# Linear attention on one core: V buffers cleared by two engines behind the first loads, the last group in another order, and two groups' stores on SyncE's queue

## The chip, the cores and the metric

The kernel runs on one core of a Trainium2 chip. The core's engines are TensorE (PE, with its weight loads shown as PEld), VectorE (DVE), ScalarE (ACT), GpSimd (POOL) and SyncE (SP); they work side by side and wait for one another through semaphores. Data move between the chip's memory (HBM) and the on-chip buffers by DMA, which an engine asks for and 16 DMA engines carry out. The metric is device time in microseconds, the median of several runs.

## The reference

For each of 8 x 12 heads, with 512 rows of 64 elements in float32:

```python
Q_feat = np.maximum(0, Q) + 1
K_feat = np.maximum(0, K) + 1
KV = np.einsum('bhkd,bhkv->bhdv', K_feat, V)
K_sum = np.sum(K_feat, axis=2)
numerator = np.einsum('bhqd,bhdv->bhqv', Q_feat, KV)
denominator = np.einsum('bhqd,bhd->bhq', Q_feat, K_sum)
return (numerator / (denominator[:, :, :, None] + 1e-10)).astype(np.float32)
```

That is attention without a softmax: one 64 x 64 product of K and V a head, applied to every row of Q and divided by a row sum. Inputs are 3 x 12.6 MB and the output 12.6 MB.

## The kernel before, in words

The rows are laid out over 128 partitions, and the work is cut into NG = 12 groups of 8 heads. A group goes through these steps:

- `load(g)`: K, Q and V come in by DMA and are turned from float32 to bfloat16 on the way; only K of group 0 comes as float32, through SP's queue. All other loads are asked for by POOL, as 1 DMA for K, 4 for V and 1 for Q. The four V pieces of 32 partitions each go into four diagonal blocks of a large tile `v_blk` (5 blocks of 2 x 16 x 64 elements); what lies off the diagonal must be zero, and the fifth block holds ones at four columns (the copy at L196), which make the row sums of K in the same matmul. There are NV = 3 such tiles, cleared once at the start on VectorE (L186), and used by groups in turn.
- `features(g)`: max(x + 1, 1) on VectorE, two instructions for K (`kf`) and two for Q (`qf`).
- `keys_values(g)`: 32 matmuls on PE into `kva_ps`, and four copies by ScalarE into a block-diagonal tile `kva_diag` (also three of them, cleared at L188).
- `transposes(g)`: 16 transposes of `qf` on PE into `qt_ps`, and two copies by ScalarE into `qt`.
- `output(g)`: four tiles of matmuls `o_ps` on PE; for each a reciprocal (L172) and a multiply (L173) on VectorE into `o_sb`. Two tiles fit in PSUM at a time, so the third waits for VectorE's multiply of the first.
- `store(g)`: `o_sb` goes out by one DMA of POOL's queue, that of the last group as two halves by SP's queue (L106).

Every engine works through its instructions in the order in which the code at the end of the kernel issues them; nothing reorders them. The loads run AHEAD = 3 groups in front, the stores LAG = 3 groups behind, and both are issued by POOL in one line, so a DMA that has to wait there holds up those behind it. The tile framework adds the waits: a V load waits for the clearing of its tile or for the matmuls that last read it, and POOL has eight semaphores for its DMAs, so that a DMA waits until the eighth before it has landed. In each round of the loop the order is features of g, transposes of g - 1, output of g - 2, keys_values of g, then the load of g + 3 and the store of g - 3. After the loop come the rest of the last three groups and four stores.

Of the kernel before, what the change touches and what calls it, by code (L numbers as in the profile page):

```python
# [8 lines left out]
FP32 = mybir.dt.float32  # L9
BF16 = mybir.dt.bfloat16  # L10
# [5 lines left out]
LAG = 3  # L16
AHEAD = 3
# [3 lines left out]
def kernel(  # L21
# [52 lines left out]
    raw = {}  # L74
    feat = {}
    qts = {}
    outs = {}

    def load(g):
        first = g == 0  # L80
        k_raw = (head_pool if first else in_pool).tile(
            [P, 2, C2, D], FP32 if first else BF16, name="k_raw"
        )
        q_raw = in_pool.tile([P, 2, C2, D], BF16, name="q_raw")
        (nc.sync if first else nc.gpsimd).dma_start(  # L85
            out=k_raw, in_=k_dram[:, g * 2 : g * 2 + 2]
        )
        if first:
            nc.gpsimd.dma_start(out=q_raw, in_=q_dram[:, g * 2 : g * 2 + 2])  # L89
        for b in range(4):  # L90
            nc.gpsimd.dma_start(  # L91
                out=v_blk[g % NV][32 * b : 32 * b + 32, b],
                in_=v_dram[32 * b : 32 * b + 32, 2 * g : 2 * g + 2],
            )
        if not first:
            nc.gpsimd.dma_start(out=q_raw, in_=q_dram[:, g * 2 : g * 2 + 2])  # L96
        raw[g] = (k_raw, q_raw)

    def store(g):
        o_sb = outs.pop(g)  # L100
        o_to = o_dram[:, g * NP : g * NP + NP]
        if g < NG - 1:
            nc.gpsimd.dma_start(out=o_to, in_=o_sb)  # L103
            return
        for h in range(2):
            nc.sync.dma_start(out=o_to[:, h:NP:2], in_=o_sb[:, h:NP:2])  # L106

    def feature(dst, src):
        nc.vector.tensor_scalar(  # L109
            out=dst, in0=src, scalar1=1.0, scalar2=1.0, op0=ALU.add, op1=ALU.max  # L110
        )

    def features(g):
        k_raw, q_raw = raw.pop(g)
        kf = feat_pool.tile([P, C2, 2, D], BF16, name="kf")
        qf = feat_pool.tile([P, C2, 2, D], BF16, name="qf")
        for n in range(2):
            feature(kf[:, :, n], k_raw[:, n])
        for half in range(2):
            cs = slice(half * C, half * C + C)  # L120
            feature(qf[:, cs].rearrange("p c n d -> p n c d"), q_raw[:, :, cs])
        feat[g] = (kf, qf)

    def keys_values(g):
        kf, _ = feat[g]
        vb = v_blk[g % NV]
        kva_ps = psum_kva.tile([P, 5, D], FP32, name="kva_ps")
        for c in range(C2):
            for n in range(2):
                nc.tensor.matmul(  # L130
                    kva_ps[64 * n : 64 * n + 64],
                    lhsT=kf[:, c, n, :],
                    rhs=vb[:, :, n, c, :],
                    start=(c == 0),
                    stop=(c == C2 - 1),
                )
        kva = kva_diag[g % NV]
        for n in range(2):
            ps = slice(64 * n, 64 * n + 64)
            nc.scalar.copy(out=kva[ps, :, n, 0:D], in_=kva_ps[ps, 0:4, :])  # L140
            nc.scalar.copy(out=kva[ps, :, n, D], in_=kva_ps[ps, 4, 0:4])  # L141

    def transposes(g):
        _, qf = feat.pop(g)
        qt = mid_pool.tile([P, C, P, 2], BF16, name="qt")
        for half in range(2):
            qt_ps = psum_qt.tile([P, C, P], BF16, name="qt_ps")
            for c in range(C):
                nc.tensor.transpose(qt_ps[:, c, :], qf[:, half * C + c, :, :], identity)  # L149
            nc.scalar.copy(out=qt[:, :, :, half], in_=qt_ps)  # L150
        qts[g] = qt
# [29 lines left out]
        outs[g] = o_sb  # L181

    with tc.manual_schedule():
        nc.vector.memset(ones, 0.0)  # L184
        for t in v_blk:
            nc.vector.memset(t, 0.0)  # L186
        for t in kva_diag:
            nc.vector.memset(t, 0.0)  # L188
        for g in range(AHEAD):
            load(g)  # L190
            if g == 0:
                make_identity(nc, identity)
                for b in range(4):
                    nc.vector.memset(ones[32 * b : 32 * b + 32, b : b + 1], 1.0)
                for t in v_blk:
                    nc.vector.tensor_copy(  # L196
                        out=t[:, 4, :, :, 0:4].rearrange("p n c j -> p (n c) j"),
                        in_=ones[:, None, :].to_broadcast([P, 2 * C2, 4]),
                    )
        for g in range(NG - 1):  # L200
            features(g)
            if g >= 1:
                transposes(g - 1)
            if g >= 2:
                output(g - 2)
            keys_values(g)
            if g + AHEAD < NG:
                load(g + AHEAD)
# [12 lines left out]

# [28 lines left out]
```

## Time and profile before

| | |
|---|---|
| Time before, median of 3 runs | 133.04 us (132.28 to 133.11) |
| Profiled execution | 131.9 us, of which span 130.1 us |
| Granted TensorE clock, mean | 0.834 |
| Busy share PE, PEld, DVE, ACT, POOL | 57%, 41%, 56%, 32%, 39% |
| HBM read and written | 37.75 MB and 12.58 MB |
| First matmul | 19.97 us |
| Last multiply on VectorE ends | 126.47 us |

The profile is one execution. Its times run from the start of the span. "Busy" is time in an instruction; what ended an engine's idle time stands behind an arrow. PEclk is the clock that TensorE was granted, as a share of full speed; the DMA row gives the mean busy share of the 16 DMA engines, and the GB/s row what they moved, counted where the data land or leave on the chip's side of the float32 to bfloat16 turn. In a timeline a row is: start, microseconds from the first to the last of its instructions, engine, line, operation, output and input, count, and in brackets the idle time ahead of it and what ended that.

### The profile page before, as it was taken

To read this page: it belongs to the slowest core of one execution; us is meant where nothing else is said; L and a number is where in the kernel's file an instruction comes from. 1 tells how busy PE (TensorE), PEld (TensorE's weight loads), DVE (VectorE), ACT (ScalarE), POOL (GpSimd) and SP (SyncE) were. 2 spreads that over 40 slices of the span, in tenths; PEclk is the share of its full clock that TensorE was granted. 3 is DMA by queue.
4 is the path that set the end of the run, shared out by engine and by line. 5 is a ranking of instruction groups with operands and counts; after the bars stand their busy time and mean duration, and the time that the engine had idled before them with its cause. 6 is when DMAs were issued, how large, how long until landed. Compare 5 with 4: busy or idle time off the path is not lost.

```text
span 130.1 us, 2367 instructions
## 1 busy us (share of the span) xinstructions
PE 74.2 (57%) x960; PEld 53.4 (41%) x960; DVE 72.7 (56%) x158; ACT 41.4 (32%) x73; POOL 51.4 (39%) x88
## 2 busy tenths in 40 slices
PE   0000008996929785694912992991992896378130
PEld 0000004674816564473811761670662664156120
DVE  4976989237486592928507607705724805990180
ACT  0000030298360739027270045046028019003600
POOL 3093773194618244462462372273273240202000
PEclk9999999999995999689997578568559559959965
DMA  3999999999999999999999999999999999999834
GB/s 86 327 152 154 205 204 203 208 212 207 212 207 212 209 208 211 207 281 303 195 248 336 207 235 348 212 222 358 205 218 354 218 212 377 419 417 413 343 154 178
DMA packets 13914, 32.13 MB, mean 247 GB/s; under 512 B 1360, under 2 KB 1360, under 8 KB 13904
## 3 DMA queue, kind: packets, MB, share of 16 engines
q0 software_dynamic: 13088, 29.89, 98.5%
q1 hardware_dynamic: 816, 2.10, 4.4%
q8 instruction: 7, 0.11, 0.3%
q14 instruction: 3, 0.02, 0.0%
HBM read 37.75 MB, written 12.58 MB: 387 GB/s over the span
## 4 chain that ended last, share of the span: by engine, by line
DMA 51%; DVE 22%; PE 12%; issue 6%; POOL 4%; ACT 2%; ACTq 1%; POOLq 0%
DMA k_raw<-in_K_dram 17%; DMA v_blk<-in_V_dram 15%; DVE v_blk L186 10%; DMA q_raw<-in_Q_dram 9%; PE kva_ps L130 9%; DMA out_dram<-o_sb 9%; DVE o_sb L173 6%; POOL v_blk L91 3%; PE o_ps L162 2%; DVE kf L109 2%; DVE qf L109 1%; DVE recip L172 1%; DVE kva_diag L188 1%; ACT qt L150 1%; PE qt_ps L149 1%
## 5 line engine op out<-in xcount | busy, mean ns | idle before, releaser
L130 PE MATMUL kva_ps<-v_blk,kf 128*64 128x320 bf16 x384 | 42.8, 396 | 20.1 <-DMA q_raw<-in_Q_dram 20.0
L130 PEld LDWEIGHTS <-kf 128*64 128x64 bf16 x384 | 28.3, 147 | 30.5 <-DVE kf L109 20.5
L162 PE MATMUL o_ps<-kva_diag,qt 128*64 128x130 bf16 x384 | 20.9, 249 | 31.2 <-DVE o_sb L173 28.1
L91 POOL DMA_DIRECT2D v_blk<-in_V_dram x48 | 25.8, 544 | 32.5 <-DMA k_raw<-in_K_dram 11.8
L173 DVE TENSOR_TENSOR o_sb<-o_ps,recip 128x512 f32<-128x512 f32 x48 | 33.2, 691 | 1.6
L150 ACT COPY qt<-qt_ps 128x1024 bf16<-128x1024 bf16 x24 | 29.6, 1302 | 0.3
L162 PEld LDWEIGHTS <-qt 128*64 128x64 bf16 x384 | 13.8, 122 | 37.1 <-DVE o_sb L173 32.7
L140 ACT CAST kva_diag<-kva_ps 64x256 bf16<-64x256 f32 x24 | 8.9, 371 | 63.3 <-PE kva_ps L130 62.9
L109 DVE TENSOR_SCALAR qf<-q_raw 128x1024 bf16<-128x1024 bf16 x24 | 9.7, 447 | 30.3 <-DMA q_raw<-in_Q_dram 30.3
L103 POOL DMA_DIRECT2D out_dram<-o_sb x11 | 8.5, 773 | 21.9 <-DVE o_sb L173 10.1
L172 DVE RECIPROCAL recip<-o_ps 128x8 f32<-128x8 f32 x48 | 9.4, 197 | 11.7 <-PE o_ps L162 11.7
L186 DVE MEMSET v_blk<- 128x5120 uint32 x3 | 13.0, 4325 | 3.1 <-issue 3.1
L149 PE MATMUL qt_ps<-identity,qf 128*128 128x128 bf16 x192 | 14.0, 231 | 0.0
L149 PEld LDWEIGHTS <-qf 128*128 128x128 bf16 x192 | 11.9, 104 | 4.2 <-issue 4.2
L109 DVE TENSOR_SCALAR kf<-k_raw 128x1024 bf16<-128x1024 bf16 (+1 forms) x24 | 9.8, 450 | 5.8 <-DMA k_raw<-in_K_dram 3.4
L85 POOL DMA_DIRECT2D k_raw<-in_K_dram x11 | 7.8, 713 | 8.2 <-DMA out_dram<-o_sb 3.7
L96 POOL DMA_DIRECT2D q_raw<-in_Q_dram x11 | 7.9, 716 | 2.9 <-DVE kf L109 1.1
L140 ACT ACT_TABLE_LOAD x1 | 1.3, 1283 | 17.5 <-DVE kva_diag L188 17.5
L141 ACT CAST kva_diag<-kva_ps 64x4 bf16<-64x4 f32 x24 | 4.0, 168 | 0.0
L188 DVE MEMSET kva_diag<- 128x520 bf16 x3 | 1.5, 492 | 0.2
L89 POOL DMA_DIRECT2D q_raw<-in_Q_dram x1 | 0.8, 823 | 0.8 <-POOLq L234 0.8
L184 DVE MEMSET ones<- 128x2 uint32 x1 | 0.1, 60 | 0.8 <-PEq L234 0.8
(8 smaller groups left out, 1.6 us busy)
## 6 DMA issues: line engine op xcount, KB each, us to landing
out_dram<-o_sb POOLq DMA_DIRECT2D x11, 1024.0 KB, 12.0
q_raw<-in_Q_dram POOLq DMA_DIRECT2D x12, 512.0 KB, 10.0
v_blk<-in_V_dram POOLq DMA_DIRECT2D x48, 128.0 KB, 9.2
k_raw<-in_K_dram POOLq DMA_DIRECT2D x11, 512.0 KB, 11.8
k_raw<-in_K_dram SPq DMA_DIRECT2D x1, 1024.0 KB, 4.9
out_dram<-o_sb SPq DMA_DIRECT2D x2, 512.0 KB, 2.7
```

The costliest lines, as they stand in the source:

```text
L91: nc.gpsimd.dma_start(out=v_blk[g % NV][32 * b : 32 * b + 32, b], in_=v_dram[32 * b : 32 * b + 32, 2 * g : 2 * g + 2],)
L96: nc.gpsimd.dma_start(out=q_raw, in_=q_dram[:, g * 2 : g * 2 + 2])
L103: nc.gpsimd.dma_start(out=o_to, in_=o_sb)
L109: nc.vector.tensor_scalar(out=dst, in0=src, scalar1=1.0, scalar2=1.0, op0=ALU.add, op1=ALU.max)
L130: nc.tensor.matmul(kva_ps[64 * n : 64 * n + 64], lhsT=kf[:, c, n, :], rhs=vb[:, :, n, c, :], start=(c == 0), stop=(c == C2 - 1),)
L140: nc.scalar.copy(out=kva[ps, :, n, 0:D], in_=kva_ps[ps, 0:4, :])
L149: nc.tensor.transpose(qt_ps[:, c, :], qf[:, half * C + c, :, :], identity)
L150: nc.scalar.copy(out=qt[:, :, :, half], in_=qt_ps)
L162: nc.tensor.matmul(ops[c // 4][64 * j : 64 * j + 64, c // 2 % 2, (c % 2) * W : (c % 2) * W + W], lhsT=qt[:, c, 32 * b : 32 * b + 32, :], r ...
L172: nc.vector.reciprocal(out=recip, in_=cells[:, :, :, :, D:D1])
L173: nc.vector.tensor_tensor(out=o_sb[:, h:NP:2, 4 * i : 4 * i + 4].rearrange("p n (b c) d -> p b c n d", b=2), in0=cells[:, :, :, :, 0:D], i ...
L186: nc.vector.memset(t, 0.0)
```

## The change

It has three parts. At the start, K and Q of groups 0 and 1 are asked for before anything is cleared; each V tile is cleared by VectorE (4/7 of its columns, as 32-bit words) and ScalarE (3/7, as a copy of a zero column) together; the `kva_diag` tiles are cleared by POOL; and the third V tile is cleared after the features of group 0. In the last group, the K features come before output of group 9, and the Q features, the K and V product and the transposes before output of group 10. The stores of group 10 go, like those of group 11, as two halves through SP's queue.

```diff
+    zero = const.tile([P, 1], FP32, name="zero")
...
-    def load(g):
+    def load_k(g):
...
+    def load_v(g):
...
+    def load_q(g):
...
     def store(g):
         o_sb = outs.pop(g)
         o_to = o_dram[:, g * NP : g * NP + NP]
-        if g < NG - 1:
+        if g < NG - 2:
             nc.gpsimd.dma_start(out=o_to, in_=o_sb)
             return
         for h in range(2):
             nc.sync.dma_start(out=o_to[:, h:NP:2], in_=o_sb[:, h:NP:2])
+    def edge(i):
+        return v_blk[i][:, 4, :, :, 0:4].rearrange("p n c j -> p (n c) j")
...
-    def features(g):
+    def k_features(g):
...
+    def q_features(g):
...
     with tc.manual_schedule():
+        nc.gpsimd.memset(zero, 0.0)
+        load_k(0)
+        load_q(0)
+        load_k(1)
+        load_q(1)
         nc.vector.memset(ones, 0.0)
-        for t in v_blk:
-            nc.vector.memset(t, 0.0)
+        for b in range(4):
+            nc.vector.memset(ones[32 * b : 32 * b + 32, b : b + 1], 1.0)
+        flat = [t.rearrange("p b n c d -> p (b n c d)").bitcast(FP32) for t in v_blk]
+        width = flat[0].shape[1]
+        part = width * 4 // 7
+        nc.vector.memset(flat[0][:, 0:part], 0.0)
+        nc.scalar.copy(
+            out=flat[0][:, part:width], in_=zero.to_broadcast([P, width - part])
+        )
+        nc.vector.tensor_copy(out=edge(0), in_=ones[:, None, :].to_broadcast([P, 2 * C2, 4]))
+        load_v(0)
...
+        make_identity(nc, identity)
         for t in kva_diag:
-            nc.vector.memset(t, 0.0)
-        for g in range(AHEAD):
-            load(g)
...
+            nc.gpsimd.memset(t, 0.0)
+        load_v(1)
+        load_k(2)
+        k_features(0)
+        q_features(0)
...
+        load_v(2)
+        load_q(2)
         for g in range(NG - 1):
-            features(g)
-            if g >= 1:
+            if g:
+                k_features(g)
+                q_features(g)
                 transposes(g - 1)
...
-        transposes(NG - 2)
-        output(NG - 3)
-        features(NG - 1)
-        output(NG - 2)
-        keys_values(NG - 1)
-        transposes(NG - 1)
-        output(NG - 1)
-        for g in range(NG - 1 - LAG, NG):
+        last = NG - 1
+        k_features(last)
+        transposes(last - 1)
+        output(last - 2)
+        q_features(last)
+        keys_values(last)
+        transposes(last)
+        output(last - 1)
+        output(last)
+        for g in range(last - LAG, NG):
             store(g)
```

On POOL, at the start of the program, the order before was this (the `v_blk` rows are four DMAs each; the number behind a name tells buffers apart):

```order
L89 DMA q_raw_103<-in_Q_dram 128x2x1024
L91 DMA v_blk0_86<-in_V_dram 32x2x1024 x4
masks.py:197 MEMSET identity_85 128x128
masks.py:199 ISA
masks.py:199 AFFINE_SELECT identity_85<-identity_85 128x128
L85 DMA k_raw_121<-in_K_dram 128x2x1024
L91 DMA v_blk1_87<-in_V_dram 32x2x1024 x4
L96 DMA q_raw_122<-in_Q_dram 128x2x1024
L85 DMA k_raw_129<-in_K_dram 128x2x1024
L91 DMA v_blk2_88<-in_V_dram 32x2x1024 x4
```

and in the changed kernel it is this:

```order
L195 MEMSET zero_90 128x1
L100 DMA q_raw_99<-in_Q_dram 128x2x1024
L86 DMA k_raw_101<-in_K_dram 128x2x1024
L100 DMA q_raw_103<-in_Q_dram 128x2x1024
L93 DMA v_blk0_86<-in_V_dram 32x2x1024 x4
masks.py:197 MEMSET identity_85 128x128
masks.py:199 ISA
masks.py:199 AFFINE_SELECT identity_85<-identity_85 128x128
L219 MEMSET kva_diag0_91 128x520
L219 MEMSET kva_diag1_92 128x520
L219 MEMSET kva_diag2_93 128x520
L93 DMA v_blk1_87<-in_V_dram 32x2x1024 x4
```

K and Q of group 1 (`k_raw_101`, `q_raw_103`) now stand ahead of the first V load, and three memsets stand between the first and the second.

On VectorE, at the end of the program, the features of the last group stood together between the outputs of groups 9 and 10 before (`o_sb_1362` is group 9's, `o_sb_1417` group 10's):

```order
L172 RECIPROCAL recip_1405<-o_ps_1387 128x8
L173 TENSOR_TENSOR o_sb_1362<-o_ps_1387,recip_1405 128x4x2x64
L172 RECIPROCAL recip_1408<-o_ps_1388 128x8
L173 TENSOR_TENSOR o_sb_1362<-o_ps_1388,recip_1408 128x4x2x64
L109 TENSOR_SCALAR kf_1411<-k_raw_1104 128x16x64 x2
L109 TENSOR_SCALAR qf_1412<-q_raw_1105 128x2x8x64 x2
L172 RECIPROCAL recip_1436<-o_ps_1418 128x8
```

Now the K features (`kf_1346`) come ahead of all of group 9's output (`o_sb_1370`), and the Q features (`qf_1419`) alone behind it:

```order
L116 TENSOR_SCALAR kf_1346<-k_raw_1109 128x16x64 x2
L183 RECIPROCAL recip_1389<-o_ps_1371 128x8
L184 TENSOR_TENSOR o_sb_1370<-o_ps_1371,recip_1389 128x4x2x64
L183 RECIPROCAL recip_1392<-o_ps_1372 128x8
L184 TENSOR_TENSOR o_sb_1370<-o_ps_1372,recip_1392 128x4x2x64
L183 RECIPROCAL recip_1413<-o_ps_1395 128x8
L184 TENSOR_TENSOR o_sb_1370<-o_ps_1395,recip_1413 128x4x2x64
L183 RECIPROCAL recip_1416<-o_ps_1396 128x8
L184 TENSOR_TENSOR o_sb_1370<-o_ps_1396,recip_1416 128x4x2x64
L116 TENSOR_SCALAR qf_1419<-q_raw_1115 128x2x8x64 x2
L183 RECIPROCAL recip_1499<-o_ps_1481 128x8
```

With this the 32 matmuls of the last K and V product and the 16 transposes, which on PE stood behind all of output of group 10, stand between the outputs of groups 9 and 10. On SP two stores follow the load of K of group 0 before, and four now.

More of the change, by code (lines that the diff above doesn't have):

```diff
@@ L71 @@
     ones = const.tile([P, 4], BF16, name="ones")
+    zero = const.tile([P, 1], FP32, name="zero")
     kva_diag = [const.tile([P, 4, 2, D1], BF16, name=f"kva_diag{i}") for i in range(NV)]
[L74 to L75 removed]
+    k_in = {}
+    q_in = {}
+    kfs = {}
+    qfs = {}
     qts = {}
     outs = {}
[L79 to L85 removed]
+    def load_k(g):
+        k_raw = (head_pool if g == 0 else in_pool).tile(
+            [P, 2, C2, D], FP32 if g == 0 else BF16, name="k_raw"
+        )
+        (nc.sync if g == 0 else nc.gpsimd).dma_start(
             out=k_raw, in_=k_dram[:, g * 2 : g * 2 + 2]
         )
[L88 to L89 removed]
+        k_in[g] = k_raw
+    def load_v(g):
         for b in range(4):
@@ L94, in load @@
             )
-        if not first:
-            nc.gpsimd.dma_start(out=q_raw, in_=q_dram[:, g * 2 : g * 2 + 2])
-        raw[g] = (k_raw, q_raw)
+    def load_q(g):
+        q_raw = in_pool.tile([P, 2, C2, D], BF16, name="q_raw")
+        nc.gpsimd.dma_start(out=q_raw, in_=q_dram[:, g * 2 : g * 2 + 2])
+        q_in[g] = q_raw
     def store(g):
@@ L111, in feature @@
         )
-    def features(g):
-        k_raw, q_raw = raw.pop(g)
+    def k_features(g):
+        k_raw = k_in.pop(g)
         kf = feat_pool.tile([P, C2, 2, D], BF16, name="kf")
-        qf = feat_pool.tile([P, C2, 2, D], BF16, name="qf")
         for n in range(2):
             feature(kf[:, :, n], k_raw[:, n])
+        kfs[g] = kf
+    def q_features(g):
+        q_raw = q_in.pop(g)
+        qf = feat_pool.tile([P, C2, 2, D], BF16, name="qf")
         for half in range(2):
@@ L121, in features @@
             feature(qf[:, cs].rearrange("p c n d -> p n c d"), q_raw[:, :, cs])
-        feat[g] = (kf, qf)
+        qfs[g] = qf
     def keys_values(g):
-        kf, _ = feat[g]
+        kf = kfs.pop(g)
         vb = v_blk[g % NV]
```

25 lines of the change are left out of this document (14 added, 11 removed).

## The prediction

> **What bounds the kernel now.** I read the page's 40 slices first, since they show whether one resource is full from end to end or only in stages.
>
> ```profile
> PEclk9999999999995999689997578568559559959965
> DMA  3999999999999999999999999999999999999834
> GB/s 86 327 152 154 205 204 203 208 212 207 212 207 212 209 208 211 207 281 303 195 248 336 207 235 348 212 222 358 205 218 354 218 212 377 419 417 413 343 154 178
> ```
>
> The digits of the DMA row look full from the second slice to the thirty-seventh, but the rates under them do not: slices 3 and 4 (6.5 to 13 us) move about 153 GB/s where the loads after them move 205 to 212, and the last two slices are low. So DMA sets the pace in the middle, and time can only be lost or won at the two edges. The windows view gives the edges in numbers (a stretch and its length, then busy time and count on PE, PEld, DVE, ACT and POOL, PEclk, DMA share and, last, GB/s).
>
> ```profile
> 7.00:12.00 5.00, 0.00 (x0) 0.00 (x0) 4.33 (x1) 0.00 (x0) 2.97 (x8) 1.00 0.92 136
> 12.00:52.00 40.00, 25.45 (x352) 18.70 (x352) 25.48 (x59) 17.69 (x31) 21.55 (x37) 0.96 1.12 208
> 108.00:122.00 14.00, 7.75 (x115) 5.46 (x112) 8.13 (x20) 5.21 (x8) 1.50 (x2) 0.88 1.03 414
> 122.00:130.00 8.00, 1.71 (x32) 1.14 (x32) 3.31 (x8) 0.51 (x1) 0.00 (x0) 0.65 0.48 187
> 128.50:129.00 0.50, 0.00 (x0) 0.00 (x0) 0.00 (x0) 0.00 (x0) 0.00 (x0) 0.50 0.42 156
> ```
>
> Two deficits can be read off. From 7 to 12 us the queues move 136 GB/s where a steady stretch of loads moves 208: (208 - 136) x 5 / 208 = **1.7 us** lost. From 122 us on, 187 x 8 = 1496 KB are left, which at the 414 GB/s of the stretch before would be done in 3.6 us, at 125.6; in fact the last bytes move at about 128.7 (156 GB/s in the half microsecond to 129.0 is 0.2 us of full rate). That is **3.1 us** lost. Behind the last byte the span runs another 1.4 us, which the change leaves alone.
>
> **Part 1: the head.** The rows around the first deficit, in order of time:
>
> ```profile
> 0.74 0.43 SPq L85 DMA_DIRECT2D k_raw<-in_K_dram  x1
> 1.27 0.82 POOL L89 DMA_DIRECT2D q_raw<-in_Q_dram  x1 [0.82 <-POOLq L234]
> 1.91 4.33 DVE L186 MEMSET v_blk<- 128x5120 uint32 x1 [1.04 <-issue]
> 6.54 2.13 POOL L91 DMA_DIRECT2D v_blk<-in_V_dram  x4 [4.45 <-DVE v_blk L186]
> 7.25 4.33 DVE L186 MEMSET v_blk<- 128x5120 uint32 x1 [1.02 <-issue]
> 9.20 0.72 POOL L85 DMA_DIRECT2D k_raw<-in_K_dram  x1
> 11.88 2.12 POOL L91 DMA_DIRECT2D v_blk<-in_V_dram  x4 [1.96 <-DVE v_blk L186]
> ```
>
> POOL has one load (Q of group 0) out at 1.27, then sits 4.45 us behind the first memset, so that K and Q of group 0 run out while V is only being asked for. Now K and Q of group 1 stand ahead of that wait: two more issues of 0.72 us behind 2.09 us, done by 3.6. They hold 2 x 524 KB, so at 208 GB/s the queue, which ran thin at about 7.5, is fed 5.0 us longer, to 12.5.
>
> V of group 0 has to be asked for before that. DVE now clears 2925 of 5120 columns. The memsets start 7.25 - 1.91 = 5.34 us apart, so 4/7 is 3.05 us (2.5 by the busy time alone, 3.5 if the 1.0 us of "issue" stays whole); behind the small memsets of the ones tile it ends near 4.4. ScalarE clears 2195 columns by an operation that the trace lacks; the bounds are from these rows:
>
> ```profile
> L150 ACT COPY qt<-qt_ps 128x1024 bf16<-128x1024 bf16 x24 | 29.6, 1302 | 0.3
> L140 ACT CAST kva_diag<-kva_ps 64x256 bf16<-64x256 f32 x24 | 8.9, 371 | 63.3 <-PE kva_ps L130 62.9
> L141 ACT CAST kva_diag<-kva_ps 64x4 bf16<-64x4 f32 x24 | 4.0, 168 | 0.0
> L140 ACT ACT_TABLE_LOAD x1 | 1.3, 1283 | 17.5 <-DVE kva_diag L188 17.5
> L109 DVE TENSOR_SCALAR kf<-k_raw 128x1024 bf16<-128x1024 f32 x2 | 1.3, 704 | 0.0
> L188 DVE MEMSET kva_diag<- 128x520 bf16 x3 | 1.5, 492 | 0.2
> masks.py:199 POOL TENSOR_SCALAR_AFFINE_SELECT identity<-identity 128x128 bf16<-128x128 bf16 x1 | 0.3, 289 | 0.1
> masks.py:197 POOL MEMSET identity<- 128x128 bf16 x1 | 0.2, 223 | 0.0
> ```
>
> (371 - 168) / 252 = 0.81 ns a column gives 1.9 us; 1302 / 1024 = 1.27 ns gives 2.8. I take the middle, 2.3, behind a table load of 1.28: done by about 4.5, at worst 5. So V is asked for near 5, against 6.54, and 7.5 us ahead of 12.5. Its four issues end near 7.1, and the queue holds work to 15.1.
>
> POOL then does what VectorE did: three memsets of 128x520. Bounds for one: 0.49 us, as on VectorE, and 289 x 520 / 128 = 1.17 us; I take 223 x 520 / 128 = 0.9, the nearest in kind. With the identity that is 3.2 us (2.0 to 4.0), and V of group 1 is asked for near 10.3 (9 to 11), against 15.1: covered. VectorE does the features of group 0 (2 x 0.70 for K, 1.0 for Q as at 112.58 below) before the third memset, so V of group 2 comes near 13.7; V of group 1 and K of group 2, at 2.5 us each, keep the queue busy to 20.1. POOL's limit of eight DMAs under way does not thin the queue: even seven V pieces and one K hold 7 x 131 + 524 KB, 6.9 us. Everything that the head adds has a cover of 3 us or more; no gap is left in the queue. Term: **-1.7**, with -1.2 and -1.75 as ends (the deficit itself is the most that can come back).
>
> PE's first matmul moves up by some 5 us, which I price at nothing by itself: in the middle DMA is full and features wait for Q anyway.
>
> **Part 2: the tail.** Times here are on the clock of before; the head's gain shifts all of them alike, since the chain hangs on loads landing.
>
> ```profile
> 46.51 2.34 PE L130 MATMUL kva_ps<-v_blk,kf 128*64 128x320 bf16 x32
> 102.42 4.48 PE L130 MATMUL kva_ps<-v_blk,kf 128*64 128x320 bf16 x32
> ...
> 102.92 0.69 DVE L173 TENSOR_TENSOR o_sb<-o_ps,recip 128x512 f32<-128x512 f32 x1
> 104.93 1.49 POOL L103 DMA_DIRECT2D out_dram<-o_sb  x2 [1.66 <-DMA k_raw<-in_K_dram]
> 108.09 0.64 PE L162 MATMUL o_ps<-kva_diag,qt 128*64 128x130 bf16 x16
> 108.55 0.21 DVE L172 RECIPROCAL recip<-o_ps 128x8 f32<-128x8 f32 x1 [4.94 <-PE o_ps L162]
> 110.37 0.42 PE L162 MATMUL o_ps<-kva_diag,qt 128*64 128x130 bf16 x8 [0.42 <-DVE o_sb L173]
> 111.30 0.69 DVE L173 TENSOR_TENSOR o_sb<-o_ps,recip 128x512 f32<-128x512 f32 x1
> 112.29 0.75 POOL L103 DMA_DIRECT2D out_dram<-o_sb  x1 [5.86 <-DVE o_sb L173]
> 112.58 1.02 DVE L109 TENSOR_SCALAR qf<-q_raw 128x1024 bf16<-128x1024 bf16 x2
> 115.76 3.27 PE L130 MATMUL kva_ps<-v_blk,kf 128*64 128x320 bf16 x32
> 118.97 1.07 PE L149 MATMUL qt_ps<-identity,qf 128*128 128x128 bf16 x16
> 119.13 0.37 ACT L140 CAST kva_diag<-kva_ps 64x256 bf16<-64x256 f32 x1 [8.74 <-PE kva_ps L130]
> 120.06 2.45 ACT L150 COPY qt<-qt_ps 128x1024 bf16<-128x1024 bf16 x2
> 123.02 0.21 DVE L172 RECIPROCAL recip<-o_ps 128x8 f32<-128x8 f32 x1 [6.07 <-PE o_ps L162]
> 124.82 2.05 SPq L106 DMA_DIRECT2D out_dram<-o_sb  x2
> 125.78 0.69 DVE L173 TENSOR_TENSOR o_sb<-o_ps,recip 128x512 f32<-128x512 f32 x1
> ```
>
> Before, VectorE waits 6.07 us, to 123.02, for the last group's product, transposes and copies; its last multiply ends at 126.47, long after the store queue has run dry. Now, step by step:
>
> - K features of group 11 go into VectorE's gap between 103.6 and 108.55. K has landed by 104.93 (POOL's wait for it ends there), and two of them take 0.85: hidden, with 2.8 us to spare.
> - Output of group 9 runs as before; its last matmuls end at 110.8, VectorE at 112.0. PE goes straight on with the last product, at 2.3 us if the granted clock is full as in the row at 46.51, so to 113.1.
> - Q features, 1.0 us, end at 113.0; the transposes, 1.1 us, at 114.2. ScalarE's copies (0.9 and 2.45) run from 113.2 to 116.6.
> - Output of group 10 starts on PE at 114.2 and on VectorE 0.46 us later (108.55 - 108.09). A group takes 111.99 - 108.55 = 3.44 there. Group 11 follows without a stop (qt is there at 116.6, wanted at 117.2), so VectorE ends near **121.5**, 5 us earlier than before.
>
> **Part 3: the stores.** Groups 5 to 9 stay on POOL's queue: 5 x 1049 KB at 414 GB/s is 12.7 us from the last load's end near 108.6, to 121.3. The four halves of groups 10 and 11 become ready near 116.4, 118.1, 119.8 and 121.5. Thus the queues are never dry, and all bytes are out at 125.6: the whole tail deficit, **-3.1**, comes back, and the last 1.6 us that compute also won stay unused. Moving group 10's store to SP I price at nothing: one queue alone already runs at 414 GB/s, and with POOL its store would be issued near 118.5, also before the backlog ends. SP waits in order for group 10, then 11, and has nothing queued behind. By the Trainium skill ("DMA: Bandwidth & Descriptors", Issuing engines are not separate DMA queues) DMAs from all issuers share the same 16 engines and only issue time is saved; that speaks against this edit, and the 414 GB/s of a single queue agrees.
>
> **Sum.** Span 130.1 - 1.7 - 3.1 = 125.3; with the 1.8 us around the span, 127.1 against the profiled execution's 131.9. That execution is 1.1 us under the median of the runs shown, 133.04; taking 4.8 us off the median gives **128.2**.
>
> **Rivals.**
> 1. The clock takes the tail. If the last product runs as at 102.42 (4.48 us, PEclk 5), the transposes at up to 1.3, VectorE ends near 123.9. The last half store then needs about 2.8 us to its last byte (126.5 to 128.7 before, with its start-up), so bytes end near 126.8: tail -1.9, time 129.4. For it: 102 to 107 was granted half clock. Against: 0.88 was granted over 108 to 122, and PE now has no stop ahead of that product. By the Trainium skill ("TensorE: Matmul & The Clock Gate", Part 1) some 3.4 us of idling halves the clock and as much work restores it; by that rule the light work of PE from 108 to 111 may or may not count as idling, and the time would be the forecast's or 129.4.
> 2. One edge does not come back: the queue has gaps in the head for a reason other than the missing requests (V pieces of 32 partitions alone), tail only: 129.9. Or the last group's operands land later than I read, head only: 131.3. The row at 112.58 shows no wait for Q of group 11, which speaks against the second.
> 3. Slower: POOL's memsets run several times longer than its two small rows suggest, beside VectorE's features. V of group 1 is then late, and DMA idles one for one once the three end later than about 13.5 (15.1 less some 1.5 from request to bytes). Each microsecond beyond costs one; to eat 4.8 us and a measurable 1.3 more they must end near 19.6, 4 us each against 0.49 on VectorE. Place: between V of groups 0 and 1; the time at 4.2 us each: about 134.9. The kva tiles also are waited for by ScalarE, not before 17 us.
> 4. The order does not do what it says: the loads wait all the same, and the last group too; no change, 133.
>
> **How the numbers follow.** Forecast 0.68 (its own range 127.3 to 129.2), rival 1 0.14, rival 2 0.11 (0.07 tail only, 0.04 head only), rival 3 0.04, no change 0.03. Down from the forecast the range takes in the lowest run of before, 132.28 - 5.1 = 127.2, and a little for a queue that runs better than 414; up it goes over rival 1 and tail only: 126.9 to 130.5. Within 1% (about what a measurement here can tell from no change) is 131.7 to 134.4. Head only at 131.3 lies so near this edge that half of it counts as same: faster 0.90, same 0.06, slower 0.04.
>
> **What would show it.** Head: from 7 to 12 us the rate is near 208 GB/s, and POOL's first V issue starts near 5. Tail: the product of the last group starts on PE right behind output of group 9; VectorE's longest wait at the end shrinks from 6.07 us to about 2.5; the rate stays above 400 until bytes end, 1.4 us before the span does. I am wrong if POOL's memsets show several microseconds each, if the window from 7 to 12 stays near 136, or if the last multiply ends within 2.8 us of the last byte.

## The result, and the profile after

| | before | after |
|---|---|---|
| Median | 132.55 us (130.41 to 133.54, 15 runs) | **127.97 us** (127.69 to 128.29, 12 runs) |
| Ratio, with its 95% interval | | 0.9732 [0.9695, 0.9768] |
| Profiled execution | 131.9 us, span 130.1 us | 127.97 us, span 126.2 us |
| Granted TensorE clock, mean | 0.834 | 0.837 |
| Last multiply on VectorE ends | 126.47 us | 117.46 us |
| Last byte of the output lands | 129.23 us | 125.26 us |

The ratio leaves out those runs of before that lie more than 1.5% above its fastest one, so it is not the quotient of the two medians. The change is worth some 4 us, and the forecast of 128.2 us held. Its terms did not all hold: in medians the head gave more than forecast, the tail gave less, and one step that was priced at nothing was worth 1.6 us.

The page of the changed kernel, the same rows as in the prediction:

```profile
PEclk9999999999985999599997568559559689998555
DMA  4999999999999999999999999999999999999992
GB/s 62 347 210 208 208 208 208 210 213 207 211 207 214 205 209 214 207 292 295 212 247 336 206 225 362 206 210 362 218 208 324 263 205 289 419 414 416 414 398 115
```

The rate of 208 now stands in slices 3 and 4 as well, and the stores end in one block of 414 to 419 GB/s, with 398 and a single low slice behind it. The windows view (the same columns as in the prediction) puts numbers to the edges:

```profile
7.00:12.00 5.00, 0.00 (x0) 0.00 (x0) 4.44 (x7) 0.89 (x1) 4.23 (x8) 1.00 1.12 211
12.00:52.00 40.00, 25.58 (x364) 19.40 (x366) 20.47 (x52) 16.60 (x30) 20.36 (x33) 0.94 1.12 209
122.50:123.00 0.50, 0.00 (x0) 0.00 (x0) 0.00 (x0) 0.00 (x0) 0.00 (x0) 0.50 1.03 397
123.00:123.50 0.50, 0.00 (x0) 0.00 (x0) 0.00 (x0) 0.00 (x0) 0.00 (x0) 0.50 0.88 340
123.50:124.00 0.50, 0.00 (x0) 0.00 (x0) 0.00 (x0) 0.00 (x0) 0.00 (x0) 0.50 0.59 229
124.00:124.50 0.50, 0.00 (x0) 0.00 (x0) 0.00 (x0) 0.00 (x0) 0.00 (x0) 0.50 0.38 147
```

From 7 to 12 us the queues move 211 GB/s instead of 136. At the end the rate does not fall off a cliff: it goes from 397 through 340 and 229 to 147 GB/s, and that slope goes with the part of the tail that did not come back (below). The head in order of time, from the timeline of the changed kernel:

```profile
1.31 0.83 POOL L100 DMA_DIRECT2D q_raw<-in_Q_dram  x1 [0.47 <-issue]
1.96 2.50 DVE L206 MEMSET v_blk<- 128x2925 f32 x1 [0.68 <-DVE ones L202]
2.03 2.02 ACT L207 COPY v_blk<-zero 128x2195 f32<-128x2195 f32 x1
2.13 0.73 POOL L86 DMA_DIRECT2D k_raw<-in_K_dram  x1
2.85 0.73 POOL L100 DMA_DIRECT2D q_raw<-in_Q_dram  x1
4.75 2.14 POOL L93 DMA_DIRECT2D v_blk<-in_V_dram  x4 [1.17 <-DVE v_blk L206]
5.05 2.50 DVE L212 MEMSET v_blk<- 128x2925 f32 x1 [0.55 <-issue]
7.42 2.04 POOL L219 MEMSET kva_diag<- 128x520 bf16 x3
9.41 1.36 POOL L93 DMA_DIRECT2D v_blk<-in_V_dram  x2
20.57 2.26 POOL L93 DMA_DIRECT2D v_blk<-in_V_dram  x4 [1.84 <-PE kva_ps L141]
```

POOL's wait ahead of the first V is down from 4.45 to 1.17 us, and by then three of its loads are already out. And the tail:

```profile
106.93 2.34 PE L141 MATMUL kva_ps<-v_blk,kf 128*64 128x320 bf16 x32
108.22 0.75 DVE L116 TENSOR_SCALAR qf<-q_raw 128x1024 bf16<-128x1024 bf16 x2
109.20 1.07 PE L160 MATMUL qt_ps<-identity,qf 128*128 128x128 bf16 x16
110.66 0.21 DVE L183 RECIPROCAL recip<-o_ps 128x8 f32<-128x8 f32 x1 [1.70 <-PE o_ps L173]
112.46 5.40 SPq L110 DMA_DIRECT2D out_dram<-o_sb  x4
116.77 0.69 DVE L184 TENSOR_TENSOR o_sb<-o_ps,recip 128x512 f32<-128x512 f32 x1
```

VectorE's longest wait at the end is 1.70 us instead of 6.07, the last product takes 2.34 us, and the last multiply ends 7.8 us ahead of the last byte instead of 2.8.

Two more readings of the traces are used below. The **lag** of two profiles is how much later the one has moved the same number of bytes as the other: it shows where in a run time is won, whatever the rates do on the way. Before lags after by 1.7 us at 12 to 14 us into the run, by 1.9 to 2.1 in the middle and by 1.85 in the store phase. The **landings** are the 16 completions of each DMA, one for each DMA engine.

### The profile page after: what moved, and what is told of

The parts are those of the page before. It is cut to its first block, busy times and chain, and to the rows that moved or that the text cites. A ratio compares the mean times of both kernels' runs of the same rounds, so it can differ in the third digit from the quotient of the medians.

```text
span 126.2 us, 2374 instructions
## 1 busy us (share of the span) xinstructions
PE 70.7 (56%) x960; PEld 52.0 (41%) x960; DVE 66.0 (52%) x155; ACT 47.1 (37%) x76; POOL 53.5 (42%) x91
## 4 chain that ended last, share of the span: by engine, by line
DMA 63%; DVE 8%; POOL 8%; PE 7%; issue 6%; POOLq 0%
DMA k_raw<-in_K_dram 28%; DMA q_raw<-in_Q_dram 25%; DMA out_dram<-o_sb 10%; DVE o_sb L184 6%; POOL v_blk L93 6%; PE kva_ps L141 4%; PE qt_ps L160 2%; POOL q_raw L100 2%; PE o_ps L173 1%; DVE recip L183 1%; POOL k_raw L86 1%; DVE qf L116 1%; POOL zero L195 0%; POOLq L107 0%; POOLq L93 0%
## 5 line engine op out<-in xcount | busy, mean ns | idle before, releaser
L141 PE MATMUL kva_ps<-v_blk,kf 128*64 128x320 bf16 x384 | 40.2, 381 | 15.8 <-DMA v_blk<-in_V_dram 15.8
L93 POOL DMA_DIRECT2D v_blk<-in_V_dram x48 | 26.5, 557 | 26.7 <-DMA k_raw<-in_K_dram 11.6
L141 PEld LDWEIGHTS <-kf 128*64 128x64 bf16 x384 | 27.6, 142 | 24.5 <-DVE qf L116 15.8
L173 PE MATMUL o_ps<-kva_diag,qt 128*64 128x130 bf16 x384 | 20.4, 245 | 30.0 <-DVE o_sb L184 29.5
L116 DVE TENSOR_SCALAR qf<-q_raw 128x1024 bf16<-128x1024 bf16 x24 | 9.2, 423 | 32.7 <-DMA q_raw<-in_Q_dram 32.7
L116 DVE TENSOR_SCALAR kf<-k_raw 128x1024 bf16<-128x1024 bf16 (+1 forms) x24 | 10.9, 493 | 11.3 <-PE qt_ps L160 5.7
L107 POOL DMA_DIRECT2D out_dram<-o_sb x10 | 7.7, 773 | 15.2 <-DMA q_raw<-in_Q_dram 7.6
L206 DVE MEMSET v_blk<- 128x2925 f32 x1 | 2.5, 2496 | 0.7 <-DVE ones L202 0.7
L224 DVE MEMSET v_blk<- 128x2925 f32 x1 | 2.5, 2496 | 0.6 <-issue 0.6
L212 DVE MEMSET v_blk<- 128x2925 f32 x1 | 2.5, 2496 | 0.6 <-issue 0.6
L219 POOL MEMSET kva_diag<- 128x520 bf16 x3 | 2.0, 717 | 0.0
L207 ACT COPY v_blk<-zero 128x2195 f32<-128x2195 f32 x1 | 2.0, 2019 | 0.0
```

Of the source, the lines that this page charges most:

```text
L93: nc.gpsimd.dma_start(out=v_blk[g % NV][32 * b : 32 * b + 32, b], in_=v_dram[32 * b : 32 * b + 32, 2 * g : 2 * g + 2],)
L116: nc.vector.tensor_scalar(out=dst, in0=src, scalar1=1.0, scalar2=1.0, op0=ALU.add, op1=ALU.max)
L141: nc.tensor.matmul(kva_ps[64 * n : 64 * n + 64], lhsT=kf[:, c, n, :], rhs=vb[:, :, n, c, :], start=(c == 0), stop=(c == C2 - 1),)
L173: nc.tensor.matmul(ops[c // 4][64 * j : 64 * j + 64, c // 2 % 2, (c % 2) * W : (c % 2) * W + W], lhsT=qt[:, c, 32 * b : 32 * b + 32, :], r ...
```

## Experiments

Each edit is told against the kernel before or the changed kernel. In the tables "end" is the end of the span.

### The parts one by one

*e1_head* has the head of the changed kernel alone. Against the changed kernel, the old order of the last group and the old store of group 10 are put back:

```diff
-        if g < NG - 2:
+        if g < NG - 1:
             nc.gpsimd.dma_start(out=o_to, in_=o_sb)
...
-        k_features(last)
         transposes(last - 1)
         output(last - 2)
+        k_features(last)
         q_features(last)
+        output(last - 1)
         keys_values(last)
         transposes(last)
-        output(last - 1)
         output(last)
```

> The head of the change alone: first loads, shared clearing and POOL's memsets as in the changed kernel, the order of the last group and the store of group 10 as before. Theory (the queue sets the time, and each edge gives its own part): the window from 7 to 12 us moves 208 GB/s or more, all loads land 1.8 to 2.0 us earlier, and the tail with its wait of VectorE for the last product stays: span 128.2, against 130.1 before and 126.2 with the whole change. Rival (the tail decides alone, an earlier head is only waited away): 130.1, with a longer wait of VectorE at the end.

*e2_tail* is the kernel before with the new order of the last group; group 10's store stays on POOL. `features` is cut into its K and its Q part for that.

```diff
...
-        transposes(NG - 2)
-        output(NG - 3)
-        features(NG - 1)
-        output(NG - 2)
-        keys_values(NG - 1)
-        transposes(NG - 1)
-        output(NG - 1)
+        k_features(last)
+        transposes(last - 1)
+        output(last - 2)
+        q_features(last)
+        keys_values(last)
+        transposes(last)
+        output(last - 1)
+        output(last)
```

> The order of the last group alone: head as before, store of group 10 whole and through POOL as before. Theory: the first deficit stays (136 GB/s from 7 to 12 us), the queue no longer runs dry at the end, and the span is 128.1 (130.1 less the 2.05 that the whole change won there) rather than the 127.0 of my prediction, because the 16 engines' last completions lie about 2 us apart when they drain a full queue. Rival (the tail's gain needs the stores on SP): 129 or more, with a gap in the DMA row ahead of the last store. Second rival (prediction's size was right and the drain is an accident of one run): 127.0.

*e3_pool10* is the changed kernel with group 10's store back on POOL (`if g < NG - 1`), and *a_again* is the changed kernel once more.

> The whole change but for the store of group 10, which goes whole through POOL as before. Theory (one queue feeds all engines, the backlog covers both ways): 126.2, within 0.3 of the changed kernel. Rival (asking in halves and on a second queue shortens the drain): 1 us or more longer, with the last store of group 10 landing last or a dip in the rate between 116 and 123 us.

> The changed kernel once more, beside its parts and on the same chip. Both theories: span 126.2 within 0.4. If the uneven end is a feature of the drain and not of one run, the rate again falls over 1.5 us (about 340, 230, 150 GB/s by half microseconds) and does not stop at once.

| | median, us | ratio to before | span, us |
|---|---|---|---|
| before (13 runs; its span is that of the first profile) | 132.77 (131.63 to 133.54) | | 130.1 |
| e1_head | 130.1 (130.03 to 130.38) | 0.9779 [0.9748, 0.981] | 128.3 |
| e2_tail | 132.63 (131.29 to 133.72) | 0.9969 [0.9924, 1.0014] | 130.2 |
| e3_pool10 | 129.44 (129.36 to 129.76) | 0.9729 [0.9698, 0.9761] | 127.7 |
| a_again | 127.68 (127.5 to 127.84) | 0.9593 [0.9562, 0.9623] | 126.1 |

By the spans the way from before to after is 130.1, less 1.8 for the head, less 0.6 for the order of the last group, less 1.6 for group 10's store on SP. The head alone does what was expected. The new order alone gains nothing that can be measured, against an expectation of the whole tail; the rival, that it needs the stores on SP, is borne out by the time. But the reason is not the rate. In e3_pool10 the last byte of SP's queue lands at 125.22 us, in a_again at 125.15: the bytes are done equally early, whether group 10 goes through POOL or through SP. The difference comes behind them. These are SP's waits in e3_pool10 (for whom, in us altogether, times, longest):

```profile
SPq L281 <- DMA out_dram<-o_sb: 6.4, 3, 4.9
SPq L281 <- PEq L281: 2.3, 2, 1.8
```

and in a_again:

```profile
SPq L281 <- DMA out_dram<-o_sb: 6.3, 4, 2.7
SPq L281 <- PEq L281: 0.7, 2, 0.5
```

L281 is the end of the program. In e3_pool10 SP has its last store home and then waits another 2.3 us for the other engines, against 0.7. The profile names PE there, whose last matmul ended at 117.1. Read from the trace's records, it is POOL: its closing instruction, which is not counted as busy, lasts until 3.40 us after the last DMA of POOL's queue has landed.

| | last POOL landing | POOL's closing ends | last SP landing | end | closes |
|---|---|---|---|---|---|
| before | 124.57 | 127.97 | 129.23 | 130.12 | SP |
| after | 121.78 | 125.14 | 125.26 | 126.17 | SP, by 0.2 |
| e2_tail | 126.07 | 129.47 | 127.57 | 130.24 | POOL |
| e3_pool10 | 123.56 | 126.96 | 125.22 | 127.73 | POOL |

So the theory taken to the next runs: the span ends at the later of last SP landing + 0.90 and last POOL landing + 4.17. With the runs below, that rule gives the span of all 14 profiles of this case to 0.03 us. In before SP's end is the later by 1.4 us, which is why the old profile shows none of it. With the new order and group 10 on POOL it turns round: e2_tail's bytes are all out by 127.57, and the end is at 130.24.

### Is it the closing of POOL's queue?

*e9_poollast* leaves all as in the changed kernel, but the very last half store goes through POOL, so that the last landing of all is on POOL's queue:

```diff
-            nc.sync.dma_start(out=o_to[:, h:NP:2], in_=o_sb[:, h:NP:2])
+            eng = nc.gpsimd if (g == NG - 1 and h == 1) else nc.sync
+            eng.dma_start(out=o_to[:, h:NP:2], in_=o_sb[:, h:NP:2])
```

> The changed kernel with the very last half store, 512 KB of group 11, through POOL in place of SP. Bytes and order of the work stay. Closing theory: that DMA lands near 125.2 as before, POOL's drain ends 3.4 us later and the program 0.8 after that: span 129.4, though the rate ends where it did. Rival (bytes alone set the end, and group 10's whole store was slow for its size): 126.1 to 126.5.

131.21 us (one run), with a span of 129.4. The last landing on POOL is at 125.28, where after's last one on SP is at 125.26, and the end is 129.45 instead of 126.17. SP's waits:

```profile
SPq L282 <- DMA out_dram<-o_sb: 8.3, 1, 8.3
SPq L282 <- PEq L282: 3.7, 2, 3.2
```

The same bytes at the same moment on the other queue cost 3.3 us; that is 4.17 less 0.90. That POOL's closing sets the end is shown; why it takes so long is not.

*e10_sponly* is the kernel before with `if g < NG - 2` in `store` and nothing else.

> The kernel before with group 10's store in two halves through SP, and nothing else. Closing theory: there SP's last landing, 129.2, closes the program and POOL's, 124.6 + 4.2, lies 1.3 us inside, so nothing is gained: same time as before. Rival (the SP queue is faster by itself): 1.5 us less.

132.78 us (130.42 to 133.68), beside 132.65 for before in the same series, ratio 0.9987 [0.9914, 1.006]: no gain, since SP's last half store closes there in any case (last landing 130.63, end 131.54; POOL's last landing 125.81). The store on SP is worth something only once the new order has taken SP's end away, and the order only once POOL's end is taken away.

*e11_tailsp* has both tail edits with the old head: e2_tail with `if g < NG - 2`.

> The change without its head: order of the last group and group 10's store on SP as in the changed kernel, the start as before. Closing theory: the last landing is the changed kernel's plus what the old head loses (1.9 us in the profile of before, up to 2.6 in that of the kernel with the new order alone): span 128.0 to 128.7, and its timed runs spread by 1 us or more as those of before do, since the spread came with the old head. Rival (the spread of before comes from TensorE's clock in the tail): they lie within 0.6 us of each other like those of the changed kernel.

130.65 us (129.97 to 131.22), beside 132.65 for before in the same series, ratio 0.9941 [0.9896, 0.9986]; span 129.4, 0.7 us above the range expected. By medians the two tail edits together are worth 2.0 us with the old head, where each alone gave nothing. The closing is as the theory has it: SP lands last at 128.53, and POOL's closing ends at 128.59. The bytes themselves were late: this run lags before by 0.75 to 0.9 us already behind the head. The old head is not one number, so this run confirms the closing but sizes the tail only roughly. Its ten runs lie 1.25 us apart, as the theory of the old head has it, and not within 0.6. The old head from 10 to 15 us, first in before and then in e2_tail:

```profile
10.00:15.00 5.00, 0.00 (x0) 0.00 (x0) 3.99 (x2) 0.00 (x0) 3.12 (x6) 1.00 0.98 178
10.00:15.00 5.00, 0.00 (x0) 0.00 (x0) 3.98 (x2) 0.00 (x0) 3.13 (x6) 1.00 0.95 145
```

### The head in halves

*e4_ahead* is the kernel before with K and Q of groups 0 and 1 asked for ahead of everything; the clearing stays on VectorE. The V part of `load` becomes `load_v` for that.

```diff
...
     with tc.manual_schedule():
+        load(0)
+        load(1)
         nc.vector.memset(ones, 0.0)
...
         for g in range(AHEAD):
-            load(g)
+            load_v(g) if g < 2 else load(g)
```

> The kernel before with one edit: K and Q of group 1 are asked for right behind K and Q of group 0, ahead of the first V load. Clearing stays whole on VectorE, the tail as before. Theory (the head's gain is a queue that is fed): 2 x 524 KB cover the wait for the first memset to 12.5 us, V of group 0 is asked for at 6.5 as before, and the window from 7 to 12 us reaches 208 GB/s: span 128.2, the whole head gain without faster clearing. Rival (the gain comes from clearing V sooner): 130.1, or at best half of the gain, 129.2.

131.13 us (129.87 to 131.71; before 132.71 in the same series), ratio 0.9871 [0.9781, 0.9962]; span 129.8 where 128.2 was expected. The windows, two rows of POOL's timeline and PE's first matmul:

```profile
7.00:12.00 5.00, 0.00 (x0) 0.00 (x0) 4.33 (x1) 0.00 (x0) 2.30 (x7) 1.00 1.12 211
28.00:34.00 6.00, 4.78 (x87) 3.76 (x84) 3.66 (x10) 3.94 (x7) 4.64 (x8) 1.00 1.09 169
```

```profile
20.06 0.73 POOL L85 DMA_DIRECT2D k_raw<-in_K_dram  x1
25.39 2.23 POOL L97 DMA_DIRECT2D v_blk<-in_V_dram  x4 [4.61 <-PE kva_ps L133]
19.97 0.47 PE L133 MATMUL kva_ps<-v_blk,kf 128*64 128x320 bf16 x1 [19.97 <-DVE kf L112]
```

In before, VectorE reaches the K features of group 0 behind the clearing of all three V tiles and of the `kva_diag` tiles, and its timeline is the same in e4_ahead:

```profile
12.59 4.33 DVE L186 MEMSET v_blk<- 128x5120 uint32 x1 [1.01 <-issue]
16.97 1.59 DVE L188 MEMSET kva_diag<- 128x520 bf16 x3
19.23 1.33 DVE L109 TENSOR_SCALAR kf<-k_raw 128x1024 bf16<-128x1024 f32 x2
```

The hole from 7 to 12 us is closed here too, at 211 GB/s, and the run is 1.9 to 2.0 us ahead of before until 27 us. Then it gives 1.2 us back. V of group 3 goes into the tile of group 0, so POOL may not ask for it before group 0's product, and that product is where it was, at 19.97: V of group 0 has landed by 15.6 (by 12.5 in before), but VectorE comes to the K features only at 19.23. Before, too, asks for V of group 3 at 25.38, but its queue is behind by those 2 us and still has Q of group 2 and K of group 3 to bring (landed at 28.11 and 30.90). Here, when POOL comes out of the 4.61 us wait, little more than K of group 3 is left (landed at 28.15); the queue runs thin, and from 28 to 34 us it moves 169 GB/s. In the changed kernel VectorE has less to clear and does the K features ahead of the third tile, the product starts at 15.81, V of group 3 is asked for at 20.57, and no such dip is seen. So the shorter clearing pays twice: for the first V, and for the V that waits for the first product. Of the 1.0 us that e4_ahead is still ahead by bytes in the store phase its span keeps 0.3: the last product, which the old tail waits for, takes 4.23 us there and 3.27 in before.

*e5_shared* is e1_head with K and Q of group 1 back behind V of group 0, K of group 2 behind Q of group 1, and all three tiles cleared at the start.

```diff
         load_k(0)
         load_q(0)
-        load_k(1)
-        load_q(1)
...
+        for i in range(NV):
...
+            if i == 0:
+                load_v(0)
+                make_identity(nc, identity)
+                load_k(1)
...
         load_v(1)
+        load_q(1)
         load_k(2)
+        load_v(2)
+        load_q(2)
         k_features(0)
         q_features(0)
...
```

> The other half of the head alone: clearing shared by VectorE and ScalarE and the kva tiles cleared by POOL, but the loads asked for in the order of before, and tail and stores as before. Theory: V of group 0 is asked for near 4.75, before Q of group 0 is through at 7.5, so the queue does not run thin there either; K of group 1 follows at 7.5 and V of group 1 near 10.5, each before the one ahead is through: rate about 205 from 7 to 12 us and span 128.3 to 128.6. So each half would do alone and together they give no more. Rival (only the order matters): 136 GB/s and 130.1.

131.05 us (130.05 to 131.39; before 132.71 in the same series), ratio 0.9882 [0.9814, 0.995]; span 129.2. Windows:

```profile
7.00:12.00 5.00, 0.53 (x3) 0.19 (x5) 4.45 (x7) 0.89 (x1) 4.92 (x11) 1.00 1.12 204
15.00:16.00 1.00, 1.00 (x15) 0.62 (x12) 0.00 (x0) 0.06 (x1) 0.71 (x3) 1.00 1.04 152
```

The faster clearing alone nearly closes the hole, leaves a small one at 15 us, and is 1.4 to 1.55 us ahead of before from there on. By bytes in the store phase the order of the loads alone keeps 1.0 us, the faster clearing alone 1.55, and both together 2.1: the halves share one deficit, and neither alone brings back all of it.

*e7_poollate* does the clearing of the `kva_diag` tiles five times over, to test how long the queue is covered:

```diff
-        for t in kva_diag:
-            nc.gpsimd.memset(t, 0.0)
+        for _ in range(5):
+            for t in kva_diag:
+                nc.gpsimd.memset(t, 0.0)
```

> The changed kernel with the three POOL memsets of the kva tiles done five times over, so V of group 1 is asked for 12 x 0.68 = 8.2 us later, near 17.6 instead of 9.4. Theory of the prediction (cover to about 13.5, then one for one): DMA stands still for about 4 us around 15 to 19 us and the span is 126.2 + 4.1 = 130.3. Rival (later loads are made up for by slack in the middle): 126.2 to 127. Second rival (no cover, every microsecond counts): 134.4.

133.49 us (one run), span 131.7: 5.5 us more than after, where 4.1 more were expected.

```profile
7.41 9.67 POOL L220 MEMSET kva_diag<- 128x520 bf16 x15
17.04 2.13 POOL L93 DMA_DIRECT2D v_blk<-in_V_dram  x4
```

```profile
7.00:12.00 5.00, 0.00 (x0) 0.00 (x0) 4.50 (x6) 0.89 (x1) 4.92 (x9) 1.00 1.13 212
15.50:18.00 2.50, 2.31 (x18) 1.86 (x20) 1.86 (x3) 0.00 (x0) 2.50 (x5) 1.00 0.00 0
20.00:25.00 5.00, 3.53 (x46) 3.29 (x46) 0.00 (x0) 3.34 (x6) 4.00 (x7) 1.00 0.98 166
```

The queue runs dry just behind 15 us, as the prediction's 15.1 has it, and stands still until 18. That stop costs 3.6 us; another 1 us goes in the thin stretch behind it, from 18 to 25 us, which makes 4.6 to 4.7 by bytes through the rest of the run. The last 0.8 us is at the very end, where the 16 pieces of the last DMA land 3.18 us apart (127.63 to 130.81) instead of 1.94 in after. This gap thus cost more than its own length.

### What the end is made of

*e6_less1mb* is the changed kernel without the store of group 8.

```diff
-            store(g)
+            if g != 8:
+                store(g)
```

> The changed kernel without the store of group 8: 1 MB of the output is never written. Theory (bytes set the end): 1049 KB at 414 GB/s less, so span 126.2 - 2.5 = 123.7; VectorE's last multiply stays at 117.5, and the last halves still find a full queue. Rival (VectorE's end at 117.5 and the latency of the last half set the end): 126.2, unchanged.

125.78 us (one run), span 124.0. One MB less is 2.2 us less, against 2.5 by 1049 KB at 414 GB/s: the end of the changed kernel is set by bytes, to the better part. In the changed kernel VectorE is done 7.8 us before the last landing, but it does not stay as far ahead here: its last multiply ends at 119.46, 2.0 us later than in after, since the product of group 10 takes 4.47 us instead of 3.21. The last half store then begins to land 2.56 us behind its issue, about as in before (2.52), where the queue was empty. So here compute has begun to hold the end as well, and may be what keeps the 2.2 from being 2.5.

What keeps the last 1 us of the forecast tail back is in the landings. Of the very last DMA, the 16 engines complete at (us):

| | first | median | last |
|---|---|---|---|
| before | 129.02 | 129.14 | 129.23 |
| after | 123.32 | 124.24 | 125.26 |

In before the queue was already empty when the last half store came, and its 16 pieces land within 0.21 us. In after it stands behind a full queue, and the engines finish 1.94 us apart. The median engine is 4.9 us earlier than before, the last one 3.97. The sloping rates above (397 to 147 GB/s) are the same thing seen from the side. The spread is not made at the end: in after the pieces of a load that lands at 25.7 us are 0.3 us apart, those of the next 1.3, and those of the store that lands at 100 us 1.8. Where the engines first part, and why, stays open.

*e8_sp9* takes more off POOL's side: the changed kernel with group 9's store on SP as well (`if g < NG - 3`).

> The changed kernel with group 9's store, too, as two halves through SP; POOL keeps groups 0 to 8. Closing theory (the program ends 0.9 us after SP's last DMA has landed or 4.2 us after POOL's last one, whichever is later; POOL then still sits in its closing drain): POOL's last landing moves from 121.3 to about 118.5, SP's stays at 125.2 as the bytes are the same, and SP already closes the changed kernel by 0.3 us: span 126.1, no gain. Rival (each store taken off POOL is worth the 1.6 us that group 10's was): 124.5.

128.54 us (128.25 to 129.23), ratio 0.9834 [0.9778, 0.9889]; span 127.4, where neither theory had it: 1.3 us more than the changed kernel's for a profile of its slowest run, 0.6 to 0.9 by medians. The timeline:

```profile
107.32 16.77 SPq L110 DMA_DIRECT2D out_dram<-o_sb  x6
114.83 0.42 PE L173 MATMUL o_ps<-kva_diag,qt 128*64 128x130 bf16 x8 [0.33 <-DVE o_sb L184]
120.49 0.69 DVE L184 TENSOR_TENSOR o_sb<-o_ps,recip 128x512 f32<-128x512 f32 x1 [5.60 <-DMA out_dram<-o_sb]
```

The first multiply of group 11 waits 5.60 us for a store to leave its buffer. The two semaphores it waits for are those of group 9's two half stores (the second lands at 120.36): in this program it is they that free the buffer that group 11 writes. In the changed kernel that multiply waits for a store of POOL that landed at 110.23, before it is wanted. The edit brought a new wait, so whether SP could carry a third group is not answered by it.

## Why the prediction was right, step by step

- **DMA sets the pace, time is at the edges.** Held. The rates in the middle are 208 and 209 GB/s, and e6_less1mb shows that bytes set the end, to the better part.
- **Head, -1.7.** The mechanism held, the size was low: e1_head's span is 1.8 shorter, the lag some 2 us. V of group 0 was asked for at 4.75 (near 5 forecast), V of group 1 at 9.41 (10.3). VectorE's part takes 3.09 us from start to start (5.05 - 1.96; 3.05 forecast), ScalarE's 2.02 (2.3) and POOL's memsets 0.72 each (0.9). In medians the head is worth more, 132.77 - 130.1 = 2.7 us: the profiled execution of before, at 131.9, was one of the better ones, and the runs with the old head scatter by 1.25 us (e11_tailsp) to 4.3 (before in the last series, 130.56 to 134.84), where e1_head stays within 0.35 (130.03 to 130.38) and the changed kernel within 0.6. Why the thin queue is at times still thinner, with POOL's issues at the same times, stays open.
- **PE's earlier first matmul, at nothing.** Failed. e4_ahead shows that a head without it gives 1.2 us back at 28 to 34 us, through V of group 3, which waits for the first product. The sum did not suffer, since the term of the head took the whole deficit as coming back anyway.
- **Tail, -3.1.** Mis-sized: 130.1 - 1.8 = 128.3 went to 126.2, which is 2.1. Compute did better than forecast: on the clock of before VectorE would have ended at 117.46 + 1.85 = 119.3, against 121.5, mostly because the product of group 10 took 3.21 us and not the 4.48 of the row at 102.42. Of the 2.1, moreover, 1.6 hang on group 10's store (next point). What failed is "all bytes are out at 125.6", and with it the sign of a rate above 400 until the bytes end. The sum ends a full queue at its full rate; the 16 engines end it 1.9 us apart, the last one 1.0 behind the median, about what the term lacks, and the last of them counts. (Part 3's own bytes do not give 125.6 either: from 121.3, groups 10 and 11 at 414 GB/s take another 5.1 us, to 126.4. The 125.6 is that of the windows, by which stores already ran at 414 GB/s from 108.0.) The Trainium skill ("DMA: Bandwidth & Descriptors", Two DMAs through the same engine are not ordered) has it that nothing orders DMAs across the 16 engines. The landings agree: the last half store's first piece lands at 123.32, ahead of the last piece of the half store before it, at 123.99.
- **Group 10's store on SP, at nothing.** Failed, and of the single steps this is the largest miss: e3_pool10 has it at 1.6 us, 1.76 by medians. The step argued by rate and by time of issue, and both were right (equal last landings at 125.2). By the Trainium skill ("DMA: Bandwidth & Descriptors", Issuing engines are not separate DMA queues) a second issuer saves no more than issue time. For the moving of the bytes these runs agree, and for the end of the program they do not: behind the last landing the program ends 3.3 us later when it is POOL's than when it is SP's.
- **"Behind the last byte the span runs another 1.4 us, which the change leaves alone."** It stayed the same by luck: counted from the last landing it is 0.9 us in both kernels, because SP closes in both. Half of the tail edit would have changed it to 2.5.
- **From the profile to the median.** The span gave 3.9 us and not 4.8; the medians differ by 4.6, because before's profiled execution lay 0.65 under its median and after's on it. For the profiled execution the sum gave 127.1, 0.9 under the 127.97 measured; the 1.1 us by which the forecast put the median above the profile made up for it, though after's profile needs no such step. That 128.2 lies so near 127.97 is luck: two misses of opposite sign.
- **Rivals.** The clock did not take the tail: the last product took 2.34 us, as in the row at 46.51. POOL's memsets were short; e7_poollate shows that rival's mechanism is real, from the point forecast (dry just behind 15 us, against 15.1), and dearer than one for one: the memsets end 3.6 us behind the 13.5 of the rival, and the span is 5.5 longer. "Tail only" and "head only" did not happen, but e2_tail shows how near a tail without gain was.

## What to carry to other kernels

Read the edges of a DMA-bound kernel by GB/s and not by busy digits, and follow an earlier load through to the next buffer that waits for its product, or the queue that was filled early only runs dry later. At the end of a program, ask for each queue when its last DMA lands and how long it takes to close; here a store through POOL had to land 3.3 us before the last one of SP to be free. And end a sum of bytes not at the full rate but with the spread of the engines behind it, here about 2 us from the first to the last in the changed kernel, of which the half from the median to the last is lost.

## What the hardware showed that was not expected

- POOL's queue closes 3.3 to 3.4 us after its last landing, in every one of these runs, and the program ends 0.8 us after that when POOL is last; with SP last it ends 0.90 to 0.93 us after the landing. None of it shows as busy time.
- The 16 engines completed the last DMA 0.2 us apart in the six profiles where it met an empty queue, and 1.7 to 3.2 us apart in the seven where it came out of a full one (1.9 in after; e6_less1mb, between the two, has 1.0).
- A queue that is only thin, not empty, is not steady: with the old head the rate from 10 to 15 us was 178 GB/s in one profile and 142 to 145 in three others, with the requests at the same times. That the scatter of the kernel before goes with its head is borne out by e1_head (0.35 us in 4 runs) and e11_tailsp (1.25 in 10); that the thin queue makes it is likely, not shown.
